# A two-block transformer forward pass: the order and the engine of the first grouped weight tiles' low parts, and the queue of the scratch writes

## The chip, the cores and the metric

The kernel runs as one program on one core of a Trainium2 chip. The metric is the device time of one execution in microseconds, as the median over several executions; lower is better.

## The reference

One sequence of 512 tokens with 1024 features passes through two blocks, all in float32.

```python
def first_block(x, c, ...):                     # two layers
    mod = silu(c) @ ada_w[layer] + ada_b[layer]           # six rows of shifts, scales, gates
    h = modulate(rms_norm(x, pre_mix_g), sh_m, sc_m)
    y = gmlp_mixer(h, ...)                                # layer 0: gelu, layer norm, causal 128x128 mixing
    y = fox_mixer(h, ..., k, v, dcum)                     # layer 1: 16 heads, causal, forget gates
    x = x + g_m * rms_norm(y, post_mix_g)
    h = modulate(rms_norm(x, pre_ffn_g), sh_f, sc_f)
    x = x + g_f * rms_norm(swiglu(h, w_gu, w_down), post_ffn_g)   # hidden width 2816
    # after layer 0: k, v, dcum = shared_kv(x, ...), one projection for the later layer

def second_block(x, p, w_in, ...):
    u = rmsnorm(x, norm_in)
    # one projection to: mLSTM q, k, v, o, z and gates; attention q, k, v, z; indexer q, k, weights
    hm = mlstm(...)                                       # 4 heads
    ha = dsa_attention(...)                               # 8 heads, keys chosen by the indexer's top 128
    h = x + concat(hm, ha) @ w_out
    h = h + (p @ w_ple) * sigmoid(h @ w_ple_gate)
    return rmsnorm(h, norm_final)
```

## The kernel before

Matrix products run in a rounded float32 format, and to keep the precision each operand is split into a high and a low part. ScalarE writes the high part of a weight tile (128x1024) as a rounded copy of the loaded tile `raw`, and another engine subtracts it from `raw` to get the low part (`wsplit`, lines 272 to 284). Each product is then three products on TensorE: high by high, high by low, low by high (`mm3`, lines 415 to 418). Which engine makes a low part follows from a running count of tiles: with `share` = 2 each second one goes to GpSimd, with 1 all, with 0 none; the others go to VectorE.

The activations h lie transposed, as 8 blocks of 128 features by 512 tokens, again as high and low parts. `gemm_a` multiplies a weight tile, held still, with h and gives 128 outputs by 512 tokens. `gemm_b` holds blocks of h still and gives 128 tokens by 512 outputs; it keeps four accumulators, one for each row block of 128 tokens. TensorE's sums lie in two sets of four banks, `acc` and `tp`.

At the end of a layer part `post` (lines 533 to 557) takes each row block's two accumulators, normalises, adds the residual, writes the new residual to memory, normalises again, and for each pair of row blocks `to_T` (lines 373 to 409) transposes the result into h for the next stage, block by block: a scaling on ScalarE (line 405 or 407), a rounding copy and a subtraction on VectorE (lines 408, 409). So the first 256 tokens of h are there before the last 256. The next `gemm_a` uses this at three places (both feed-forward blocks and the indexer projection `w_ix`): its first four weight tiles are a group, whose products are done first for tokens 0 to 255 of all four tiles, then for tokens 256 to 511 (`halves`, lines 427 to 438). Within a half, tile follows tile, and each tile runs all its k blocks with all three products. The low parts of these four tiles go to GpSimd (`gshare` = 1).

DMAs are all issued by SP, in one queue, in order: weight tiles into four `raw` buffers, rows that are broadcast, and writes and reads of scratch memory. Besides the residuals these are: the copies of x transposed for a later layer (`spill`, xT), the keys of the first attention as stacks of high and low halves (`spread`, four DMAs of 256 KB for each pair of heads), half of the values (line 1078), and the queries and keys of the second attention (lines 1271, 1272 and `spread`). They are loaded again when their heads come up.

The order of each engine's instructions is made by a planner, which takes the program's order as priority and its own costs as times. An instruction that waits stops what is queued behind it on its engine, and on SP its DMAs.

Of the kernel before, what the change touches and what calls it, by code (L numbers as in the profile page):

```python
# [20 lines left out]
P = 128  # L21
T_ = 512
NT = 4
# [168 lines left out]
def body(tc, nc, a):  # L192
    V, S_, G, PE = nc.vector, nc.scalar, nc.gpsimd, nc.tensor

    with ExitStack() as es:
# [176 lines left out]
        def to_T(ts, xn, g, sh, hi, lo, js=range(KD), spill=None):  # L372


            n = len(ts) * P
            c = slice(ts[0] * P, ts[0] * P + n)
            per = 512 // n
            for q, j in enumerate(js):
                if q % per == 0:
                    pt = tp()  # L380
                    f = None
                src = pt[:, (q % per) * n:(q % per + 1) * n]
                for i, t in enumerate(ts):
                    PE.transpose(src[:, i * P:(i + 1) * P], xn[t][j // 4][:, (j % 4) * P:(j % 4 + 1) * P], ident[:])  # L384
                if g is None:
                    S_.activation(hi[j][:, c], src, AF.Copy)
                    V.tensor_sub(lo[j][:, c], src, hi[j][:, c].bitcast(F32))
                    continue
                if spill is not None and q % per == per - 1:
                    raw, f = T(), T()  # L390
                    part = [(j - per + 1 + i, slice(i * n, (i + 1) * n)) for i in range(per)]
                    for i, s in part:
                        S_.activation(f[:, s], pt[:, s], AF.Identity, scale=g[:, i:i + 1], bias=sh[:, i:i + 1])
                    V.tensor_copy(raw, pt)
                    nc.sync.dma_start(spill[j - per + 1:j + 1, :, c].rearrange("j p n -> p j n"), b3(raw, per))
                    for i, s in part:
                        V.tensor_copy(hi[i][:, c], f[:, s])
                        V.tensor_sub(lo[i][:, c], f[:, s], hi[i][:, c].bitcast(F32))
                if spill is not None:
                    continue  # L400
                if f is None:
                    f = T()
                fj = f[:, (q % per) * n:(q % per + 1) * n]
                if sh is None:
                    S_.activation(fj, src, AF.Copy, scale=g[:, j:j + 1])
                else:
                    S_.activation(fj, src, AF.Identity, scale=g[:, j:j + 1], bias=sh[:, j:j + 1])
                V.tensor_copy(hi[j][:, c], fj)  # L408
                V.tensor_sub(lo[j][:, c], fj, hi[j][:, c].bitcast(F32))  # L409
# [10 lines left out]
        def gemm_a(h, w, n, evac, m=P, group=0, nfill=0, share=0, gshare=1):  # L420


            hi, lo = h
            i = 0
            while i < n:
                run = list(range(i, min(n, i + (group if i == 0 and group else 1))))
                halves = (slice(0, 256), slice(256, 512)) if i == 0 and group else (slice(0, 512),)
                ws, accs = [], []
                for q in run:
                    ws.append(wsplit(w[q], KD * m, gshare if len(run) > 1 else share))  # L430
                    accs.append(acc())
                    if len(run) == 1:
                        fill(nfill if i >= 10 or not group else 0)
                for c in halves:
                    for (wh, wl), pt in zip(ws, accs):
                        for k in range(KD):
                            mm3(pt[0:m, c], wh[:, k * m:(k + 1) * m], wl[:, k * m:(k + 1) * m],
                                hi[k][:, c], lo[k][:, c], k == 0, k == KD - 1)
                for q, pt in zip(run, accs):
                    evac(q, pt)  # L440
                i += len(run)
# [92 lines left out]
        def post(gb, xsrc, xdst, alloc, done):  # L534
# [4 lines left out]
            def evac(g, t, pt):  # L539
# [3 lines left out]
                if g == 1:  # L543
# [6 lines left out]
                    rsq(r, r, 1.0 / D)  # L550
                    for h in range(2):
                        V.scalar_tensor_tensor(xr[h], yg[t, h], r, xr[h], ALU.mult, ALU.add)
                        nc.sync.dma_start(xdst[rows, h * 512:(h + 1) * 512], xr[h])
                    xn = [yg[t, 0], yg[t, 1]]
                    norm_rows(xr, xn)
                    done(t, xn)
# [362 lines left out]
        def spread(d, at, hi, lo):  # L919

            for q, (src, half) in zip(at, ((hi, TOP), (lo, TOP), (hi, BOT), (lo, BOT))):
                nc.sync.dma_start(d[q].rearrange("(a p) n -> p a n", a=2),
                                  src[half].unsqueeze(1).broadcast_to((64, 2, 512)))

        def loader(alloc, src, n, last):

# [122 lines left out]
        with tc.tile_pool(name="x", bufs=1) as px:  # L1049
# [24 lines left out]
            def vdone(q, t, o):  # L1074
                if q < 2:
                    vt_[t, q] = o
                else:
                    nc.sync.dma_start(vscr[(q - 2) * NT + t], o.bitcast(F32))
            gemm_b(hk, a["w_k"], range(2), KD, headnorm(kt_, ka, kdone), head=True, share=KS, hshare=KH)
            dcol = []  # L1080
            dscr = scratch([16, 512])
# [115 lines left out]
        with tc.tile_pool(name="z", bufs=NZ) as pz:  # L1197
# [65 lines left out]
            def ev_a(i, pt):  # L1263
# [4 lines left out]
                if i % 2 == 0:  # L1268
                    for q, half in enumerate((TOP, BOT)):
                        ot = (BOT, TOP)[q]  # L1270
                        nc.sync.dma_start(d[3 * q, half], hi[half])
                        nc.sync.dma_start(d[3 * q, ot], lo[half])
                else:
                    spread(d, (1, 2, 4, 5), hi, lo)
            gemm_a(h, a["w_aqk"], 2, ev_a, share=2)
# [343 lines left out]
```

## Time and profile before

| | before |
|---|---|
| time, median of 3 runs | 1910.1 us (1907.51 to 1917.22) |
| profiled execution: its time | 1910.77 us |
| profiled execution: span | 1908.9 us |
| mean granted TensorE clock | 0.983 |
| VectorE busy | 1130.9 us (59%) |
| ScalarE busy | 792.2 us (41%) |
| GpSimd busy | 375.9 us (20%) |
| moved by DMA | 305.75 MB, all but some 1.5 MB on the one queue |

The span runs from the first instruction's start to the last one's end. A stretch is busy for an engine where an instruction of it runs; matmuls overlap, so their busy time is no measure of rate, and the number of matmuls in a stretch is counted as well. The granted clock is a share of TensorE's full speed.

### The profile page before, as it was taken

The page shows a single profiled execution, that of the slowest core. Times are in us where ns is not written, and L with a number is a line of the kernel's source. Part 1 is how long each engine was busy: PE and PEld are TensorE (multiplying, and loading weights), DVE is VectorE, ACT ScalarE, POOL GpSimd, SP SyncE. Part 2 cuts the span into 40 slices and gives each one's busy share as a digit, 9 for nine tenths or more (in the row PEclk, how much of TensorE's full clock was granted, in tenths as well). Part 3 has the DMA queues.
Part 4 walks back from the last instruction along what each step waited for, and adds up shares of the span by engine and source line. Part 5 has one row for each costly group of instructions (what it writes and reads, how often), then busy time and mean ns, then how long its engine had stood idle before and what let it go on. Part 6 is the DMA issues. An engine that isn't in the chain of part 4 may idle for free. (4 is left out here: it accounts for less than half of the span.)

```text
span 1908.9 us, 23835 instructions
## 1 busy us (share of the span) xinstructions
PE 1832.5 (96%) x8688; PEld 1514.8 (79%) x8688; DVE 1130.9 (59%) x2132; ACT 792.2 (41%) x1395; POOL 375.9 (20%) x216
## 2 busy tenths in 40 slices
PE   8899989999999999799998999999989999999998
PEld 5788877888888877587777888888878888888887
DVE  7879844677772256439876433232267978846534
ACT  5334324423232245448764422222246246455334
POOL 2100122222220012344323111100020363031011
PEclk9999999999999999899998999999989999999999
DMA  8684752477773444855533222222434744332522
GB/s 336 235 280 134 238 207 83 158 266 271 249 253 107 136 144 145 265 177 157 185 100 111 92 97 99 97 98 103 144 116 134 231 143 135 105 105 89 192 90 100
DMA packets 109647, 305.75 MB, mean 160 GB/s; under 512 B 12277, under 2 KB 15133, under 8 KB 109530
## 3 DMA queue, kind: packets, MB, share of 16 engines
q1 hardware_dynamic: 109530, 304.23, 47.8%
q8 instruction: 69, 1.13, 0.2%
q14 instruction: 48, 0.39, 0.1%
HBM read 269.50 MB, written 37.30 MB: 161 GB/s over the span
## 5 line engine op out<-in xcount | busy, mean ns | idle before, releaser
L279 ACT ACTIVATE whi<-raw 128x1024 fp32r<-128x1024 f32 x293 | 309.9, 1059 | 672.0 <-PE acc L418 295.9
L282 POOL TENSOR_TENSOR wlo<-raw,whi 128x1024 fp32r<-128x1024 f32 x124 | 305.2, 2465 | 1348.5 <-ACT whi L279 1062.2
L417 PE MATMUL acc<-h,whi 128*128 128x512 f32 (+1 forms) x1112 | 417.3, 375 | 10.4 <-DVE h L409 10.2
L416 PE MATMUL acc<-h,whi 128*128 128x512 f32 (+1 forms) x1112 | 417.6, 376 | 5.8 <-DVE h L408 5.2
L418 PE MATMUL acc<-h,wlo 128*128 128x512 f32 (+1 forms) x1112 | 416.0, 374 | 0.6 <-POOL wlo L282 0.6
L282 DVE TENSOR_TENSOR wlo<-raw,whi 128x1024 fp32r<-128x1024 f32 x169 | 214.4, 1271 | 299.2 <-ACT whi L279 294.7
L416 PE MATMUL acc<-whi,h 128*128 128x512 f32 x608 | 241.4, 398 | 19.5 <-ACT whi L279 12.2
L417 PEld LDWEIGHTS acc<-h,whi 128*128 128x128 f32 x1112 | 212.3, 191 | 48.2 <-DVE h L409 12.7
L416 PEld LDWEIGHTS acc<-h,whi 128*128 128x128 f32 x1112 | 212.4, 191 | 42.1 <-DVE h L408 6.0
L417 PE MATMUL acc<-wlo,h 128*128 128x512 f32 x608 | 240.0, 395 | 4.8 <-DVE wlo L282 3.3
L418 PEld LDWEIGHTS acc<-h,wlo 128*128 128x128 f32 x1112 | 212.4, 191 | 37.2 <-POOL wlo L282 1.0
L418 PE MATMUL acc<-whi,h 128*128 128x512 f32 x608 | 240.2, 395 | 0.0
L416 PE MATMUL acc<-whi,s 128*128 128x512 f32 (+1 forms) x488 | 190.5, 390 | 0.7 <-DVE t L1305 0.7
L302 DVE SCALAR_TENSOR_TENSOR raw<-raw,cact 128x1024 f32<-128x1024 f32 x96 | 146.7, 1535 | 74.8 <-DMA raw<-in_ada 68.2
L417 PE MATMUL acc<-wlo,s 128*128 128x512 f32 (+1 forms) x488 | 190.7, 391 | 0.0
L418 PE MATMUL acc<-whi,s 128*128 128x512 f32 (+1 forms) x488 | 190.2, 390 | 0.0
L416 PEld LDWEIGHTS acc<-whi,h 128*128 128x128 f32 x608 | 115.2, 190 | 44.3 <-ACT whi L279 12.6
L417 PEld LDWEIGHTS acc<-wlo,h 128*128 128x128 f32 x608 | 115.2, 190 | 29.2 <-DVE wlo L282 4.1
L418 PEld LDWEIGHTS acc<-whi,h 128*128 128x128 f32 x608 | 115.2, 190 | 26.0 <-DVE h L409 3.0
L416 PEld LDWEIGHTS acc<-whi,s 128*128 128x128 f32 x488 | 91.7, 188 | 20.0 <-DVE t L1305 1.1
L417 PEld LDWEIGHTS acc<-wlo,s 128*128 128x128 f32 x488 | 91.7, 188 | 18.8
L418 PEld LDWEIGHTS acc<-whi,s 128*128 128x128 f32 x488 | 91.7, 188 | 18.8
(349 smaller groups left out, 2395.4 us busy)
## 6 DMA issues: line engine op xcount, KB each, us to landing
raw<-in_ada SPq DMA_DIRECT2D x96, 512.0 KB, 3.7
raw<-in_w_gu SPq DMA_DIRECT2D x88, 512.0 KB, 3.7
raw<-in_w_dn SPq DMA_DIRECT2D x44, 512.0 KB, 3.2
scr<-t SPq DMA_DIRECT2D x72, 256.0 KB, 3.8
raw<-in_w_o SPq DMA_DIRECT2D x20, 512.0 KB, 3.3
row<-scr SPq DMA_DIRECT2D x36, 256.0 KB, 3.3
d<-in_ada SPq DMA_DIRECT2D x16, 512.0 KB, 5.5
raw<-in_w_v SPq DMA_DIRECT2D x16, 512.0 KB, 5.1
```

The lines of the kernel that those rows point to most:

```text
L279: S_.activation(hi[:, 0:n], raw[:, 0:n], AF.Copy)
L282: e.tensor_sub(lo[:, 0:n], raw[:, 0:n], hi[:, 0:n].bitcast(F32))
L302: V.scalar_tensor_tensor(raw, raw, 1.0, cact[0], ALU.mult, ALU.mult, accum_out=modc[:, col:col + 1])
L416: PE.matmul(out, lh, rh, start=start, stop=False)
L417: PE.matmul(out, lh, rl, start=False, stop=False)
L418: PE.matmul(out, ll, rh, start=False, stop=stop)
```

## The change

There are two parts.

In `gemm_a` the group of four tiles is written out by itself. All four tiles are loaded and their high parts made. Then, for tokens 0 to 255, the loop over k is the outer one and the tiles the inner: for each k block and tile the two products that need only the high part of the weights (high by high, high by low). After these, tile by tile, VectorE makes the tile's low part and TensorE adds the eight products with it. Tokens 256 to 511 follow in the same order, with the low parts already there. A bank's first product alone starts the sum. The group's tiles no longer advance the running count of `wsplit`. The tile after the group sums into a bank of `tp` instead of `acc`.

The writes of the residuals, of xT, of the keys, of the values and of the second attention's queries and keys are issued by GpSimd instead of SP.

```diff
-                    nc.sync.dma_start(spill[j - per + 1:j + 1, :, c].rearrange("j p n -> p j n"), b3(raw, per))
+                    nc.gpsimd.dma_start(spill[j - per + 1:j + 1, :, c].rearrange("j p n -> p j n"), b3(raw, per))
...
-                halves = (slice(0, 256), slice(256, 512)) if i == 0 and group else (slice(0, 512),)
                 ws, accs = [], []
-                for q in run:
-                    ws.append(wsplit(w[q], KD * m, gshare if len(run) > 1 else share))
-                    accs.append(acc())
-                    if len(run) == 1:
-                        fill(nfill if i >= 10 or not group else 0)
-                for c in halves:
-                    for (wh, wl), pt in zip(ws, accs):
+                if len(run) == 1:
+                    ws.append(wsplit(w[i], KD * m, share))
+
+                    accs.append(tp() if group and i == group else acc())
+                    fill(nfill if i >= 10 or not group else 0)
+                    for k in range(KD):
+                        mm3(accs[0][0:m], ws[0][0][:, k * m:(k + 1) * m], ws[0][1][:, k * m:(k + 1) * m],
+                            hi[k], lo[k], k == 0, k == KD - 1)
+                else:
+                    raws = []
+                    for q in run:
+                        accs.append(acc())
+                        raws.append(load_w(w[q], KD * m))
+                        ws.append([tile_of(pw, q_, F32R, 1024) for q_ in ("whi", "wlo")])
+                        S_.activation(ws[-1][0], raws[-1], AF.Copy)
+
+                    for nh, c in enumerate((slice(0, 256), slice(256, 512))):
                         for k in range(KD):
-                            mm3(pt[0:m, c], wh[:, k * m:(k + 1) * m], wl[:, k * m:(k + 1) * m],
-                                hi[k][:, c], lo[k][:, c], k == 0, k == KD - 1)
+                            for (wh, _), pt in zip(ws, accs):
+                                PE.matmul(pt[:, c], wh[:, k * P:(k + 1) * P], hi[k][:, c], start=nh == k == 0, stop=False)
+                                PE.matmul(pt[:, c], wh[:, k * P:(k + 1) * P], lo[k][:, c], start=False, stop=False)
+                        for (wh, wl), pt, raw in zip(ws, accs, raws):
+                            if nh == 0:
+                                V.tensor_sub(wl, raw, wh.bitcast(F32))
+                            for k in range(KD):
+                                PE.matmul(pt[:, c], wl[:, k * P:(k + 1) * P], hi[k][:, c], start=False,
+                                          stop=nh == 1 and k == KD - 1)
...
-                        nc.sync.dma_start(xdst[rows, h * 512:(h + 1) * 512], xr[h])
+                        nc.gpsimd.dma_start(xdst[rows, h * 512:(h + 1) * 512], xr[h])
...
-                nc.sync.dma_start(d[q].rearrange("(a p) n -> p a n", a=2),
-                                  src[half].unsqueeze(1).broadcast_to((64, 2, 512)))
+                nc.gpsimd.dma_start(d[q].rearrange("(a p) n -> p a n", a=2),
+                                    src[half].unsqueeze(1).broadcast_to((64, 2, 512)))
...
-                    nc.sync.dma_start(vscr[(q - 2) * NT + t], o.bitcast(F32))
+                    nc.gpsimd.dma_start(vscr[(q - 2) * NT + t], o.bitcast(F32))
...
-                        nc.sync.dma_start(d[3 * q, half], hi[half])
-                        nc.sync.dma_start(d[3 * q, ot], lo[half])
+                        nc.gpsimd.dma_start(d[3 * q, half], hi[half])
+                        nc.gpsimd.dma_start(d[3 * q, ot], lo[half])
```

## Rows read from the trace of the kernel before

**Rows 1.** The page: share of TensorE; then groups of instructions, busy us, mean ns.

```profile
PE 1832.5 (96%) x8688; PEld 1514.8 (79%) x8688; DVE 1130.9 (59%) x2132; ACT 792.2 (41%) x1395; POOL 375.9 (20%) x216
...
L282 POOL TENSOR_TENSOR wlo<-raw,whi 128x1024 fp32r<-128x1024 f32 x124 | 305.2, 2465 | 1348.5 <-ACT whi L279 1062.2
...
L282 DVE TENSOR_TENSOR wlo<-raw,whi 128x1024 fp32r<-128x1024 f32 x169 | 214.4, 1271 | 299.2 <-ACT whi L279 294.7
```

**Rows 2.** Stretches, us: length, then each engine's busy us (x instructions), clock, DMA share.

```profile
326.50:359.60 33.10, 28.54 (x210) 26.85 (x209) 24.86 (x42) 16.09 (x30) 10.73 (x5) 0.90 0.36 119
1030.60:1066.30 35.70, 29.36 (x209) 27.75 (x209) 25.27 (x43) 15.98 (x30) 10.41 (x5) 0.86 0.32 111
...
351.00:359.00 8.00, 8.00 (x69) 8.00 (x69) 5.35 (x4) 5.97 (x7) 2.41 (x1) 1.00 0.25 76
...
330.30:337.00 6.70, 4.73 (x18) 4.11 (x18) 6.23 (x10) 2.54 (x6) 4.05 (x2) 0.50 0.47 145
```

**Rows 3.** Timeline of VectorE in the first start: begin us, duration us, line, operation.

```profile
324.85 2.88 DVE L552 SCALAR_TENSOR_TENSOR s<-t,sm,s 128x512 f32<-128x512 f32 x1
327.65 2.60 DVE L409 TENSOR_TENSOR h<-t,h 128x256 fp32r<-128x256 f32 x1
330.17 2.43 DVE L408 CAST h<-t 128x256 fp32r<-128x256 f32 x1
332.52 0.74 DVE L552 SCALAR_TENSOR_TENSOR s<-t,sm,s 128x512 f32<-128x512 f32 x1
333.19 0.41 DVE L409 TENSOR_TENSOR h<-t,h 128x256 fp32r<-128x256 f32 x1
...
338.07 0.68 DVE L542 TENSOR_TENSOR t<-acc,gb 128x512 f32<-128x512 f32 x1
...
343.96 0.29 DVE L408 CAST h<-t 128x256 fp32r<-128x256 f32 x1 [0.62 <-ACT t L407]
```

**Rows 4.** Timeline of GpSimd in the first start.

```profile
324.72 7.73 POOL L282 TENSOR_TENSOR wlo<-raw,whi 128x1024 fp32r<-128x1024 f32 x3 [18.55 <-ACT whi L279]
```

**Rows 5.** Timeline of ScalarE in the first start: the fourth high part.

```profile
333.98 1.04 ACT L279 ACTIVATE whi<-raw 128x1024 fp32r<-128x1024 f32 x1
```

**Rows 6.** Timeline of TensorE, first start and key projection; in brackets idle before, releaser.

```profile
330.30 0.58 PE L417 MATMUL acc<-h,whi 128*128 128x256 f32 x1 [1.51 <-DVE h L409]
...
332.65 0.58 PE L416 MATMUL acc<-h,whi 128*128 128x256 f32 x1 [1.55 <-DVE h L408]
...
709.09 0.79 PE L417 MATMUL acc<-wlo,h 128*128 128x512 f32 x1 [1.95 <-DVE wlo L282]
```

**Rows 7.** Timelines of TensorE, ScalarE and VectorE in the value projection.

```profile
790.78 1.22 PE L416 MATMUL acc<-whi,h 128*128 128x512 f32 x2 [12.18 <-ACT whi L279]
...
789.67 1.06 ACT L279 ACTIVATE whi<-raw 128x1024 fp32r<-128x1024 f32 x1 [0.24 <-DMA raw<-in_w_vv]
...
770.53 0.42 DVE L1102 TENSOR_SCALAR q<-q 16x512 f32<-16x512 f32 x1
```

**Rows 8.** SP's queue: begin us, us to the last issue's end, DMA, number.

```profile
730.45 3.65 SPq L271 DMA_DIRECT2D raw<-in_w_vv  x3
737.29 41.27 SPq L922 DMA_DIRECT2D scr<-t  x32
...
783.52 10.30 SPq L271 DMA_DIRECT2D raw<-in_w_vv  x5
...
762.89 15.67 SPq L922 DMA_DIRECT2D scr<-t  x16
...
699.70 0.33 SPq L553 DMA_DIRECT2D scr<-s  x1
```

**Rows 9.** Stretches, as in rows 2: value projection, two for comparison.

```profile
778.30:803.50 25.20, 11.50 (x39) 8.60 (x38) 15.87 (x30) 13.90 (x21) 11.72 (x5) 0.66 0.78 271
762.00:778.00 16.00, 16.00 (x74) 13.27 (x74) 5.98 (x9) 6.33 (x8) 0.00 (x0) 1.00 0.80 221
1100.00:1200.00 100.00, 100.00 (x443) 82.84 (x442) 33.83 (x32) 28.97 (x38) 14.36 (x6) 1.00 0.29 95
```

## The prediction, made before the changed kernel ran

> **What bounds the kernel now.** I read the page's engine shares first: TensorE is busy 96% of the span [rows 1]. So only a stretch where TensorE waits, or runs at the lower of its two clocks, can give time back. Then the table of stretches, for the three places where a group of four weight tiles begins a stage (both feed-forward blocks and the indexer projection) [rows 2]. Each holds about 208 short products and transposes; the first takes 33.1 us, the other two 35.7 each. Where the same 256-column products run undisturbed, 69 take 8.00 us, 0.116 each, so 208 want 24.1 us. The excess is 9.0 + 11.6 + 11.6 = 32.2 us. Inside the first lie 6.7 us at a granted clock of 0.50, the 1.2 GHz level; the other two have such a spell as well.
>
> The timeline of VectorE in the first of them tells why [rows 3]. Three operations in a row take 2.88, 2.60 and 2.43 us; the same forms take 0.74, 0.41 and 0.29 a little later. In just that time GpSimd makes three low parts of the group, 7.73 us together [rows 4]. VectorE loses 2.14 + 2.19 + 2.14 = 6.5 us, so with the fourth low part about 8.6. ScalarE's squares wait for it, and behind them stands the copy of the fourth high part, which starts at 333.98 [rows 5]. TensorE meanwhile stands 1.51 and 1.55 us for VectorE's activation parts [rows 6].
>
> The one large wait of TensorE is elsewhere: 12.18 us, up to 790.78, for a high part in the value projection [rows 7]. SP's queue shows the cause: three loads of w_vv, then 32 writes of keys over 41.27 us, and only at 783.52 the other five loads [rows 8]; between them stand a write of the forget gate and eight reads of xT. The high part starts as its load lands [rows 7]. From 778.3 to 803.5 TensorE did 39 products, which at 443 per 100 us want 8.8 us: 16.4 us of excess, the wait and a mean clock of 0.66 [rows 9].
>
> **Part 1, the grouped tiles.** The products are the same in number and size (4 x 2 x 8 x 3 = 192), only in another order. What goes: 3 x 4 low parts of GpSimd. What comes: 12 low parts on VectorE, 1.27 us each [rows 1], 5.1 us per start, ready from the moment the high parts are. Without GpSimd's passes the first L552 in [rows 3] ends at 325.6 and the second about 327, so the squares and the four high parts follow one another on ScalarE and the fourth is ready near 329.8 (before: 335.0). TensorE enters the group at 326.5, needs all four within its first step of k, and so idles about 2.6 us; then 62 products run 7.2 us to 337.0 and the 32 with low parts 3.7 us to 340.7. The low parts are due from 337.0 on and have 7 us on a VectorE with gaps.
>
> What is late next: the other two row blocks. Now 5.9 us pass from the last block's L542 to its first activation part [rows 3]; without the 8.6 us that L542 can start near 330.4 instead of 338.07, so the part is there at 336.3, or at 341.4 if all four low parts stand ahead of it. TensorE asks for it at 340.7: 0 to 0.7 us. After that TensorE takes 0.93 us a step of k (8 products) and VectorE 0.7 (0.29 + 0.41): no more waits. I leave 2.6 + 0.5 us of waiting and 0.9 for a spell of low clock, 4.0 per start: 32.2 - 12.0 = 20 us won. Bounds: nothing won, if the 5.1 us hit the chain and the rest comes back as another wait; 32 with no wait left. The fifth tile gets a bank of the other set, so that it need not wait for the four accumulators that now end together; cost nothing, hidden behind its own 24 products.
>
> A side effect in the code: the grouped tiles no longer count in the turn that hands low parts to GpSimd. By lines 280 and 281 the first group of the key projection then gives one tile of four to GpSimd instead of two, and the second feed-forward block 14 instead of 13: GpSimd's low parts go from 124 to 112, VectorE's from 169 to 181. In the key projection that takes one of two slowdowns of VectorE away (2.1 us) and adds a 1.27; I count 0, and what can come back at most is a wait like the 1.95 us there for VectorE's low part [rows 6].
>
> **Part 2, the writes.** 112 DMAs move: 32 of residuals, 8 of spills, 32 of keys, 8 of values, 32 of the second attention's operands. SP then loads, apart from the small writes that stay (the gate's among them). In the value projection the fourth w_vv load can go as soon as its buffer is free; by the code that is when w_f, split beside the first key pairs near 740, is done with its own. The next limit is the gate's write, which holds SP until its source is there (770.5 + 0.4) [rows 7]; loads that come free before it can be out by then. So the 12.18 us and the low clock behind them go: 16.4.
>
> What takes their place is GpSimd's queue. All low parts of w_vv and w_q are made there, in turn with the writes. The second 16 key writes start at 762.89 and took 15.67 us on SP, 0.98 each [rows 8]. The fifth low part gets its buffer in the middle of them (the first w_vv tile is done at about 767) and is due one tile after the present wait begins, 778.4 + 24 x 0.227 = 783.9. If it comes behind all 16, TensorE waits where 762.9 + 16X + 2.4 passes 783.9, from X = 1.16 us per write. The trace has no DMA issued by GpSimd. From below, a plain write costs SP 0.33 us of queue [rows 8]; from above, a GpSimd pass over 128x1024 costs 2.47 [rows 1]. I take 1.2, near the 0.98 of these same writes: 0.6 us of wait. I count 15 of the 16.4; bounds 0 and 16.4, and worse in the other-side rival below.
>
> The other moved writes: residuals and spills stand on GpSimd's queue where, but for one key tile, it now has nothing else; each waits for VectorE there and holds only later low parts. The 8 values, some 8 us at 0.98, stand among low parts that come every 5.45 us and take 2.4, so 3 us are free per tile, and three tiles of lead cover the 8. The 32 operand writes come at four per tile of products, by 0.98 four of 5.45 us. I add 1 us for all of it, bounds -1 and +10.
>
> **Sum.** The profiled execution took 1910.8 us (span 1908.9), 0.7 above the median of 1910.1. 1910.8 - 20 - 15 + 1 = 1876.8, say 1877.
>
> **Rivals.**
> *GpSimd's queue is the new bound in the value projection.* At X = 2.0 the wait is 16 x 0.84 = 13.4 us and the second part wins nothing; with part 1 intact 1910.8 - 20 + 1 = 1892. For it: VectorE is busy 5.98 of 16.0 us there [rows 9]; if a write rests while VectorE works, 0.98 becomes 1.56, a wait of 6.4 us, and 1883. Against: three tiles of lead. The Trainium skill speaks for it: in "SBUF — State Buffer", section "SBUF: two separate sides", a DMA from GpSimd's queue has its descriptors written by that engine, which is locked out of the shared port while VectorE copies in a fast mode, and the advice is to issue from SP or ScalarE. The slowdowns of [rows 3] agree with a port held for a whole instruction; no row shows a descriptor being written. Chance 0.13.
>
> *The loads stay late.* SP keeps the order gate, xT, w_vv; the wait at 790 remains and only part 1 works: 1892. For it: that order now [rows 8]; against: three w_vv loads go even ahead of the writes. Chance 0.09.
>
> *The low parts land in VectorE's chain.* Then 5.1 us per start come off, 15 of the 20: 1892. For it: they are ready early and the engine is in order; against: VectorE waits for ScalarE several times in each block, and low parts fit there. Chance 0.11.
>
> *The other side: a write holds GpSimd and slows VectorE for as long as a low part does, 2.4 us.* Four residual writes in each start then replace the four low parts and cost the same 8.6 us, VectorE's own 5.1 come on top (3 x 5.1 = 15), and the value projection waits 16 x 1.24 = 20 us, 4 over its excess now: 1910.8 + 15 + 4 = 1930. It decides from where 12 writes in the starts and 16 in the value projection eat the 36 us: 12X + 16(X - 1.16) = 36, X = 1.95. Against: SP's writes cost a third to a half of that. Chance 0.09.
>
> **How the numbers follow.** Forecast 0.55, with its own range 1862 to 1890 (12 us less won, or the waits of part 1 gone too). The three middle cases 0.33, near 1892 alone and near 1907 two at once; the other side 0.09; better than 1862 0.03. The range 1862 to 1906 leaves out that 0.03 and, above, the other side and some of the pairs. A change under 0.5% (9.6 us) can't be told from none: faster is the forecast and most of the middle cases, 0.79; same 0.11, the pairs; slower 0.10.
>
> **What would show it.** VectorE's operations in the three starts back at 0.3 to 0.8 us; those stretches at 26 to 30 us; the fourth w_vv load before 771 and no wait over 3 us before the fifth tile's products; a mean granted clock above the 0.983 of now. Wrong would be: writes of 2 us on GpSimd, or low parts there that end after TensorE asks for them.

## The result and the profile after

The changed kernel takes 1891.0 us (median of 4 runs, 1888.4 to 1893.7) where the kernel before, beside it, takes 1912.3: a ratio of 0.9878, with a 95% interval of 0.9857 to 0.9898. The forecast was 1877. The gain is 21 us; the forecast, made against the profiled 1910.8, had 34.

The profiled execution took 1890.45 us, with a span of 1888.6 us and a mean granted clock of 0.989. Both kernels do the same 8,688 products and transposes in nearly the same order, so the time from the start of the n-th to that of the m-th compares a stage across traces. From the start times, in us (the row "end of the program" is from the end of ScalarE's last output scaling to the end of the span):

| stretch (n to m) | before | after | difference |
|---|---|---|---|
| first start, feed-forward 1 (1300 to 1500) | 39.9 | 32.2 | -7.7 |
| late tiles of feed-forward 1 (2100 to 2650) | 124.9 | 130.3 | +5.4 |
| down and key projection (2650 to 3190) | 125.1 | 122.5 | -2.6 |
| value projection (3190 to 3600) | 110.1 | 109.3 | -0.8 |
| second start, feed-forward 2 (4500 to 4800) | 55.3 | 45.2 | -10.1 |
| third start and the rest of the indexer (6250 to 6800) | 110.1 | 102.5 | -7.6 |
| end of the program | 3.8 | 6.7 | +3.0 |
| all other stretches together | | | +0.1 |

The sum is -20.3, the difference of the two spans. So the starts gave more than was forecast, and the value projection gave nothing.

The page of the kernel after answers to [rows 1]: GpSimd makes 112 low parts; VectorE's 169 and the group's 12 on a line of their own make 181.

```profile
PE 1823.4 (97%) x8688; PEld 1506.0 (80%) x8688; DVE 1116.9 (59%) x2144; ACT 789.8 (42%) x1395; POOL 409.1 (22%) x316
...
L282 POOL TENSOR_TENSOR wlo<-raw,whi 128x1024 fp32r<-128x1024 f32 x112 | 273.3, 2443 | 893.3 <-ACT whi L279 825.9
L282 DVE TENSOR_TENSOR wlo<-raw,whi 128x1024 fp32r<-128x1024 f32 x169 | 214.7, 1273 | 301.8 <-ACT whi L279 278.8
```

The table of stretches of the kernel after, columns as in [rows 2]: the three starts, and the value projection.

```profile
328.20:353.70 25.50, 25.45 (x210) 24.92 (x209) 16.78 (x41) 13.71 (x29) 3.15 (x4) 1.00 0.39 127
1026.50:1052.00 25.50, 25.46 (x209) 24.84 (x208) 16.80 (x40) 13.62 (x28) 4.02 (x4) 1.00 0.37 125
1391.70:1417.20 25.50, 25.50 (x210) 25.02 (x209) 17.25 (x41) 12.41 (x26) 3.13 (x4) 1.00 0.49 158
757.50:781.50 24.00, 9.41 (x30) 7.25 (x29) 11.88 (x13) 9.58 (x13) 20.26 (x21) 0.64 0.86 283
```

Each start is a solid 25.5 us at full clock, where [rows 2] has 33.1 and 35.7. VectorE's timeline in the first start (begin, duration) shows why: the forms that took 2.88 and 2.60 us in [rows 3] are back at 0.75 and 0.42, and the four low parts of 1.2 us lie between them.

```profile
326.54 0.75 DVE L568 SCALAR_TENSOR_TENSOR s<-t,sm,s 128x512 f32<-128x512 f32 x1
327.21 0.42 DVE L409 TENSOR_TENSOR h<-t,h 128x256 fp32r<-128x256 f32 x1
...
328.95 1.22 DVE L451 TENSOR_TENSOR wlo<-raw,whi 128x1024 fp32r<-128x1024 f32 x1
```

In the value projection the wait is still there, with another name. TensorE's timeline of the kernel after, to be read beside [rows 7]:

```profile
773.01 0.80 PE L417 MATMUL acc<-wlo,h 128*128 128x512 f32 x1 [14.59 <-POOL wlo L282]
```

GpSimd's timeline says what that low part waited for (in brackets: idle before, and what ended it):

```profile
735.31 4.78 POOL L938 DMA_DIRECT2D scr<-t  x8 [0.16 <-issue]
...
743.64 0.60 POOL L938 DMA_DIRECT2D scr<-t  x1 [1.85 <-DMA scr<-t]
...
758.73 0.60 POOL L938 DMA_DIRECT2D scr<-t  x1 [10.06 <-ACT t L1081]
...
769.99 0.60 POOL L938 DMA_DIRECT2D scr<-t  x1 [0.15 <-issue]
770.60 9.32 POOL L282 TENSOR_TENSOR wlo<-raw,whi 128x1024 fp32r<-128x1024 f32 x4
```

All 32 key writes stand ahead of the first low part of w_vv. A write holds the queue only 0.60 us, but the later ones of the first 16 wait until an earlier write has landed (0.24 to 1.85 us each), and the second 16 wait 10.06 us for their data. SP did what was forecast, up to a point: four w_vv loads went out by 737, but the other four again only at 784.79. Their buffers come free from 773.0 on, as the low parts are made, but reads of xT stand ahead of them on SP, and the last four of these waited for buffers of their own until 782.25. TensorE did not wait for these loads.

```profile
727.13 9.83 SPq L271 DMA_DIRECT2D raw<-in_w_vv  x4
...
782.25 2.45 SPq L1125 DMA_DIRECT2D t<-scr  x4
784.79 1.90 SPq L271 DMA_DIRECT2D raw<-in_w_vv  x4
```

### The profile page after: what moved, and what is told of

It reads as the page before. It is cut to its first block, busy times and chain, and to the rows that moved or that the text cites. A ratio compares the mean times of both kernels' runs of the same rounds, so it can differ in the third digit from the quotient of the medians.

```text
span 1888.6 us, 23901 instructions
## 1 busy us (share of the span) xinstructions
PE 1823.4 (97%) x8688; PEld 1506.0 (80%) x8688; DVE 1116.9 (59%) x2144; ACT 789.8 (42%) x1395; POOL 409.1 (22%) x316
## 5 line engine op out<-in xcount | busy, mean ns | idle before, releaser
L279 ACT ACTIVATE whi<-raw 128x1024 fp32r<-128x1024 f32 x281 | 296.7, 1058 | 661.4 <-PE acc L418 302.1
L282 POOL TENSOR_TENSOR wlo<-raw,whi 128x1024 fp32r<-128x1024 f32 x112 | 273.3, 2443 | 893.3 <-ACT whi L279 825.9
L418 PE MATMUL acc<-h,wlo 128*128 128x512 f32 x896 | 350.0, 391 | 3.0 <-DVE wlo L282 3.0
L416 PE MATMUL acc<-h,whi 128*128 128x512 f32 x896 | 350.8, 392 | 0.8 <-DVE s L903 0.5
L417 PE MATMUL acc<-h,whi 128*128 128x512 f32 x896 | 349.6, 390 | 0.0
L418 PEld LDWEIGHTS acc<-h,wlo 128*128 128x128 f32 x896 | 168.6, 188 | 40.2 <-DVE wlo L282 5.1
L416 PEld LDWEIGHTS acc<-h,whi 128*128 128x128 f32 x896 | 168.7, 188 | 36.9 <-issue 1.7
L302 DVE SCALAR_TENSOR_TENSOR raw<-raw,cact 128x1024 f32<-128x1024 f32 x96 | 151.6, 1589 | 76.6 <-DMA raw<-in_ada 75.2
L417 PEld LDWEIGHTS acc<-h,whi 128*128 128x128 f32 x896 | 168.5, 188 | 34.4
```

The source lines that it names most:

```text
L279: S_.activation(hi[:, 0:n], raw[:, 0:n], AF.Copy)
L282: e.tensor_sub(lo[:, 0:n], raw[:, 0:n], hi[:, 0:n].bitcast(F32))
L302: V.scalar_tensor_tensor(raw, raw, 1.0, cact[0], ALU.mult, ALU.mult, accum_out=modc[:, col:col + 1])
L416: PE.matmul(out, lh, rh, start=start, stop=False)
L417: PE.matmul(out, lh, rl, start=False, stop=False)
L418: PE.matmul(out, ll, rh, start=False, stop=stop)
```

## The experiments

Each run is compared with the kernel before on its own chip (1916 to 1917 us for e1 to e12, the 1912.3 above for the changed kernel). "Value stretch" and "late tiles" are the stretches of the table above; the undisturbed value stretch would be some 94 us, 110.1 less the 16.4 of [rows 9].

| run | ratio to before, 95% interval | value stretch | late tiles |
|---|---|---|---|
| changed kernel | 0.9878 (0.9857 to 0.9898) | 109.3 | 130.3 |
| e1 group only | 0.9885 (0.9859 to 0.9912) | 110.2 | 131.3 |
| e2 writes only | 1.0038 (1.0018 to 1.0057) | 108.3 | 129.1 |
| e3 w_vv's low parts on VectorE | 0.9868 (0.9844 to 0.9893) | 105.2 | 131.6 |
| e4 group's low parts on GpSimd | 1.0063 (1.0038 to 1.0088) | 108.4 | 132.6 |
| e5 keys written once, as e3 | 0.9827 (0.9802 to 0.9853) | 101.0 | 132.0 |
| e6 keys written once | 0.9839 (0.9822 to 0.9855) | 100.9 | 127.1 |
| e7 xT after values, as e3 | 0.9834 (0.9817 to 0.9852) | 103.2 | 133.8 |
| e8 columns from tile 6 | 0.9895 (0.9881 to 0.9910) | 108.8 | 134.4 |
| e9 xT read early, as e3 | 0.9796 (0.9778 to 0.9813) | 94.2 | 128.7 |
| e10 keys once, xT early | 0.9823 (0.9806 to 0.9841) | 101.6 | 129.3 |
| e11 as e10, low parts on VectorE | 0.9814 (0.9799 to 0.9828) | 96.2 | 131.0 |
| e12 as e9, fewer columns | 0.9924 (0.9900 to 0.9948) | 93.7 | 151.7 |

### The two parts apart

e1 takes the group and puts the writes back on SP; e2 is the kernel before with the writes on GpSimd.

```diff
# e1, at all six places
-nc.gpsimd.dma_start(...)
+nc.sync.dma_start(...)
```

> The changed kernel with all writes issued by SP again: part 1 alone. By the stretches of the changed kernel's trace against the one before, the three group starts gave 7.6 + 10.3 + 10.4 = 28.3 us, of which the later tiles of the first feed-forward block took 5.4 back and the end of the indexer projection 3.2, so part 1 is worth some 20 net. Theory (part 1 is right whole, part 2 gave nothing): 1891 +- 3, TensorE's wait of 12 us for a high part of w_vv is back near 770, the late waits for VectorE's low parts near 505 to 566 stay, since the loads of that block run at their own pace. Rival (the writes on GpSimd cost something elsewhere, and the late waits come from them): 1884 to 1886 and no waits there. Rival (the writes on GpSimd gave a share of the 21): 1895 or more.

> The kernel before with only the queue of the writes changed: part 2 alone. Theory (in the value projection the wait only changes its cause, from a late load to low parts that stand behind the 32 key writes on GpSimd's queue): 1909 to 1913, no difference from before that can be told; a wait of 13 to 16 us for GpSimd's low part near 765. Rival (the writes pay, but only because the low parts of the group no longer stand among them, or the reverse, they hold the group's low parts): the three starts change by more than 2 us each and the time leaves 1905 to 1917.

e1 measured 0.9885, the changed kernel 0.9878, with overlapping intervals: part 1 is the whole gain, as far as can be told, and part 2 on top of it nothing. TensorE's wait in the value projection is that of [rows 7] again:

```profile
792.06 1.22 PE L416 MATMUL acc<-whi,h 128*128 128x512 f32 x2 [12.05 <-ACT whi L279]
```

e2 is slower than before by 0.4%, not equal, and its value projection waits 14.3 us for GpSimd's low part, as expected. Of the rival there is something too: its first start grew by 2.6 us (42.5 against 39.9), the other two did not. It loses more in the late tiles (+4.2) and at the end of the program (+3.3), and wins 1.8 in the value projection. GpSimd's and TensorE's timelines of e2 in the first start:

```profile
327.07 2.47 POOL L282 TENSOR_TENSOR wlo<-raw,whi 128x1024 fp32r<-128x1024 f32 x1 [6.42 <-ACT whi L279]
330.38 0.56 POOL L553 DMA_DIRECT2D scr<-s  x1 [0.85 <-DVE s L552]
...
334.76 4.65 POOL L282 TENSOR_TENSOR wlo<-raw,whi 128x1024 fp32r<-128x1024 f32 x2
```

```profile
339.76 0.58 PE L417 MATMUL acc<-h,whi 128*128 128x256 f32 x1 [4.47 <-DVE h L409]
```

A residual write waits for VectorE, and the next low part, queued behind it, starts late and then slows VectorE late. The changed kernel avoids that because no low part of the group is on GpSimd's queue.

### The engine or the order of the products

```diff
-V.tensor_sub(wl, raw, wh.bitcast(F32))
+G.tensor_sub(wl, raw, wh.bitcast(F32))
```

> The changed kernel with the group's twelve low parts back on GpSimd, in the new order of the products (products with the low parts last). It tells the order from the engine. Theory (GpSimd's passes made VectorE's steps of 0.3 to 0.7 us last 2.4 to 2.9, and the starts waited for these): VectorE's steps in the starts are at 2.4 to 2.9 us again while GpSimd makes low parts, and 12 to 20 of the 28.3 us are lost: 1903 to 1911. Rival (the order is what counts: TensorE asks for the low parts later, so it does not matter who makes them): 1889 to 1894, the same as the changed kernel.

The whole gain is lost, and more: 1.0063, the first start at 42.8 us, the second at 55.8, the indexer at 113.6. VectorE's, GpSimd's and TensorE's timelines of e4:

```profile
328.69 2.90 DVE L568 SCALAR_TENSOR_TENSOR s<-t,sm,s 128x512 f32<-128x512 f32 x1
...
335.99 5.24 DVE L409 TENSOR_TENSOR h<-t,h 128x256 fp32r<-128x256 f32 x1
```

```profile
328.56 2.48 POOL L451 TENSOR_TENSOR wlo<-raw,whi 128x1024 fp32r<-128x1024 f32 x1 [6.42 <-ACT whi L442]
...
336.29 4.64 POOL L451 TENSOR_TENSOR wlo<-raw,whi 128x1024 fp32r<-128x1024 f32 x2
```

```profile
343.16 0.66 PE L384 MATMUL tp<-ident,t 128*128 128x128 f32 x2 [7.09 <-DVE t L370]
```

A step of 0.42 us lasts 5.24 while GpSimd makes two low parts, and ends 0.3 us after them. TensorE then waits 7.09 us for the chain behind that step. Residual writes stand between the low parts on GpSimd's queue here, as in e2, so e2 is the run to compare for the order alone: both have low parts and writes on GpSimd, and its starts take 42.5, 54.9 and 110.2 us, its ratio is 1.0038. The new order with GpSimd wins nothing on that. From e4 to the changed kernel only the engine differs, and the first start falls from 42.8 to 32.2. So in the new order the engine is what counts. Whether VectorE's low parts would give as much in the old order no run shows.

### What holds the value projection

e3 takes w_vv's low parts off GpSimd's queue.

```diff
-VS = 1
+VS = 0
```

> The changed kernel with the eight low parts of w_vv made by VectorE instead of GpSimd; everything else as changed. Theory (order on GpSimd's queue: the low parts wait behind 32 writes, each of which holds the queue only some 0.6 us, so a low part that is not on that queue is there when its high part is): the 14.6 us wait and the lower clock behind it go, 14 to 17 us, less 1 to 3 for eight passes of 1.2 us more on VectorE: 1875 to 1878. Rival (the loads stay late all the same, behind the gate's write on SP's queue): the wait comes back for a high part some 20 us later, 5 to 12 us, 1882 to 1890. Rival (VectorE is the bound there when it makes keys, values and low parts): waits for its low parts of over 5 us, 1885 or more.

The wait for the low part is gone, but the time hardly moves: 0.9868 against 0.9878, with overlapping intervals. The theory had 14 us more, and neither rival names what came. TensorE now waits 11.2 us for its accumulators, which ScalarE and VectorE copy out (v). TensorE's and ScalarE's timelines of e3:

```profile
792.92 0.77 PE L416 MATMUL acc<-whi,h 128*128 128x512 f32 x1 [11.21 <-DVE v L903]
```

```profile
779.40 0.82 ACT L1126 ACTIVATE t<-t,modc,gcol 128x512 f32<-128x512 f32 x1 [6.10 <-DMA t<-scr]
...
783.72 0.81 ACT L1126 ACTIVATE t<-t,modc,gcol 128x512 f32<-128x512 f32 x1 [1.21 <-DMA t<-scr]
...
787.64 0.36 ACT L901 ACTIVATE v<-acc 128x256 fp32r<-128x256 f32 x1
```

The copies (L901) are queued behind scalings of xT (L1126), and these wait for their reads. The table of stretches of e3, columns as before with the DMA share second to last, the line of its xT reads (KB, median us to landing) and SP's queue (begin, us to the last issue's end) bear on why the reads are late:

```profile
755.00:765.00 10.00, 10.00 (x52) 7.32 (x51) 9.22 (x14) 5.38 (x9) 2.59 (x5) 1.00 0.97 333
765.00:775.00 10.00, 10.00 (x46) 8.27 (x45) 5.18 (x8) 6.75 (x7) 5.88 (x10) 1.00 1.01 331
```

```profile
t<-scr SPq DMA_DIRECT2D x8, 256.0 KB, 9.0
```

```profile
762.52 0.37 SPq L1125 DMA_DIRECT2D t<-scr  x1
...
770.34 5.29 SPq L1125 DMA_DIRECT2D t<-scr  x3
...
781.47 4.63 SPq L1125 DMA_DIRECT2D t<-scr  x4
```

The 16 DMA engines are full, and a read takes 9.0 us (median of the three whose landing the trace shows). SP also issues the reads late: they stand behind weight loads, and their nine buffers `t` are shared with the keys that are being written (SP waits 5.6 us until VectorE has split earlier reads, 2.2 until key writes have landed). Two causes were set against each other: the bytes, or the order on ScalarE's queue. The late issue was not tried by itself. e5 and e6 cut the bytes: each key half is written once, 128 KB instead of 256, and read back twice.

```diff
-nc.gpsimd.dma_start(d[q].rearrange("(a p) n -> p a n", a=2),
-                    src[half].unsqueeze(1).broadcast_to((64, 2, 512)))
+nc.gpsimd.dma_start(kscr[pr, q], src[half])
...
-nc.sync.dma_start(got[p_][q].bitcast(F32), src[p_, q])
+for s in halves:
+    nc.sync.dma_start(got[p_][q].bitcast(F32)[s], src[p_, q])
```

> The kernel with w_vv's low parts on VectorE, and each key half written once (32 writes of 128 KB instead of 256) and read back twice, by 64 reads of 128 KB in place of 32 of 256: the bytes written fall by 4.2 MB, the bytes read stay. In the run with only the low parts moved, the DMA engines were busy 0.97 to 1.01 in each of the four slices from 745 to 785, the xT reads took 9.0 us to land, ScalarE's scalings of xT waited for them and TensorE waited 11.2 us for accumulators that are copied out behind these. Theory (the stretch is held by what the 16 DMA engines can move, 330 GB/s there): 4.2 MB less is 12.7 us less, so that wait falls below 3 us: ratio to the kernel before 0.977 to 0.982 (that of the run with the low parts alone was 0.987). Rival (an order on a queue, ScalarE's or SP's, holds the stretch whatever the bytes): the same wait within 3 us and 0.985 to 0.989. Rival (64 reads of 128 KB instead of 32 cost more on SP's queue, in the first attention): 0.987 or more, with new waits between 800 and 1020.

> The changed kernel with each key half written once, as in the run beside it, but w_vv's low parts still on GpSimd behind these writes. It tells the order on GpSimd's queue from the bytes. Theory (both: the writes hold the low parts because each waits until earlier ones have landed, 6.9 us apiece with 1.00 of the DMA engines busy): the writes go through in about half the time, the wait of 14.6 us for GpSimd's low part falls to 4 to 8 us: ratio 0.981 to 0.985. Rival (queue order alone; the low parts wait for the last key's data, not for the DMA engines): the wait stays over 11 us, 0.986 to 0.989. Rival (bytes alone): the wait is gone, 0.978 to 0.981, as good as the run beside it.

e5 took away only 4.5 of the 11.2 us: the same wait, 6.7 us, with the DMA share at 0.61 and 0.85 in the two stretches shown for e3. The theory of the bytes had put it below 3. e6 came out as expected in time, but not for the reason given: with smaller writes the planner put w_vv's first four low parts between the first and the second 16 writes, so order and bytes changed together. Its wait of 5.6 us is the one for the accumulators as well. GpSimd's timeline of e6:

```profile
738.25 2.08 POOL L1086 DMA_DIRECT2D scr<-t  x4 [0.84 <-DMA scr<-t]
740.35 2.40 POOL L282 TENSOR_TENSOR wlo<-raw,whi 128x1024 fp32r<-128x1024 f32 x1
...
758.82 4.19 POOL L1086 DMA_DIRECT2D scr<-t  x8
```

e7 tried the order by moving the reads and scalings of xT behind the value projection in the program.

```diff
-<the loop over j: read xT[j], scale, split>
 gemm_b(hk, a["w_vv"], ...)
+<the loop over j: read xT[j], scale, split>
```

> The kernel with w_vv's low parts on VectorE, full key writes, and the eight reads and scalings of xT put behind the value projection in the program, so that ScalarE's copies out of the accumulators no longer stand behind scalings that wait for a read. It tells the queue order on ScalarE from the bytes. Rival (order on ScalarE's queue): the wait of 11.2 us for the accumulators goes, 0.979 to 0.982. Theory (bytes: the DMA engines are full from 745 to 785 and something must come late): what is read late is late elsewhere, w_vv's later tiles or the query projection's operands, waits of 5 to 11 us in sum: 0.983 to 0.988.

It tells little: the planner still set the scalings between the copies, and TensorE waited 9.5 us for the accumulators, as ScalarE's timeline of e7 shows.

```profile
789.24 0.81 ACT L1127 ACTIVATE t<-t,modc,gcol 128x512 f32<-128x512 f32 x1 [2.90 <-DMA t<-scr]
789.96 0.36 ACT L901 ACTIVATE v<-acc 128x256 fp32r<-128x256 f32 x1
```

e9 takes away what the scalings wait for: xT is read before the key projection, into the buffers that later take the low part of the query operand. Low parts on VectorE, key writes full.

```diff
+hx = [[tile_of(px, "hm", F32R, bufs=16) for _ in range(KD)] for _ in range(2)]
+for j in range(KD):
+    nc.sync.dma_start(hx[1][j].bitcast(F32), xT[j])
 gemm_b(hk, a["w_k"], ...)
...
-    nc.sync.dma_start(f, xT[j])
-    S_.activation(f, f, AF.Identity, ...)
+    S_.activation(f, hx[1][j].bitcast(F32), AF.Identity, ...)
```

> The kernel with w_vv's low parts on VectorE and full key writes, but the eight reads of xT issued before the key projection, into the buffers of the query operand's low part; the scalings on ScalarE stay where they were. It tells whether the wait of 11.2 us near 781, for accumulators whose copies stand on ScalarE's queue behind scalings that wait for a read of xT, is one of that queue or of the bytes. By the stretch from product 3190 to 3600 (105.2 us in the run with the low parts alone, 109.3 in the changed kernel, 110.1 before), an undisturbed one would take 94. Theory (the reads land late because the DMA engines are full, and ScalarE's order hands that on to TensorE; read early, 2 MB leave the full stretch and nothing in front of the copies waits): no wait over 3 us from 735 to 805, the stretch at 94 to 97 us, ratio to the kernel before 0.978 to 0.982. Rival (bytes: something else of the 17 MB that stay comes late, a w_vv or w_q tile): a wait of 5 to 10 us for a high part, 100 to 105 us, 0.983 to 0.987.

This one shows what TensorE waits for. The value stretch is 94.2 us, with two waits of 2.0 us together, and the ratio 0.9796, faster than both kernels. The table of stretches of e9:

```profile
745.00:755.00 10.00, 10.00 (x46) 7.03 (x45) 6.43 (x9) 7.47 (x13) 0.60 (x1) 1.00 0.95 332
755.00:765.00 10.00, 10.00 (x52) 8.23 (x51) 8.72 (x13) 7.10 (x10) 4.78 (x8) 1.00 0.99 345
765.00:775.00 10.00, 10.00 (x46) 8.28 (x45) 8.65 (x17) 8.93 (x12) 5.12 (x8) 1.00 0.99 331
```

The DMA engines are as full as in e3 and the key writes as large, and TensorE does not wait in these 30 us. So full DMA engines are not what holds it: the late reads are, and the order on ScalarE's queue hands their lateness on, as its timeline of e3 shows. What made the reads late is not shown. e9 has SP issue them between 716.76 and 724.24, into other buffers, and so takes away the late issue and the slow landing at once.

e10 and e11 join both cures, with w_vv's low parts on GpSimd and on VectorE.

> The changed kernel (w_vv's low parts on GpSimd) with each key half written once and the xT reads issued before the key projection. Theory (the wait of 5.5 us that was left with the keys written once was only that of the late xT reads): stretch from product 3190 to 3600 at 94 to 97 us, no wait over 3 us from 735 to 805, ratio to the kernel before 0.977 to 0.981, some 1874 to 1880 where before has 1916. Rival (the low parts on GpSimd still come behind the key writes): a wait for GpSimd's low part of 3 us or more, 98 to 101 us, 0.982 to 0.984.

> As the run beside it (keys written once, xT read early), with w_vv's low parts on VectorE. Theory: once neither the writes nor the xT reads hold anything, it does not matter who makes these low parts: the stretch at 94 to 97 us and a time within 0.2% of the run beside it. Rival (eight passes of 1.2 us are too many for VectorE beside key and value work): a wait for VectorE's low part or for its copies of 2 us or more, 0.2 to 0.4% slower than the run beside it. Rival (the low parts on GpSimd slow VectorE there): 0.2 to 0.4% faster.

e10 has the rival's time (101.6 us, 0.9823) by another way. No low part comes late; TensorE waits 6.17 us for the accumulators. VectorE's and GpSimd's timelines of e10:

```profile
767.84 3.07 DVE L1131 CAST hm<-t 128x512 fp32r<-128x512 f32 x1 [0.28 <-ACT t L1130]
770.83 3.50 DVE L1132 TENSOR_TENSOR hm<-t,hm 128x512 fp32r<-128x512 f32 x2
```

```profile
768.19 2.42 POOL L282 TENSOR_TENSOR wlo<-raw,whi 128x1024 fp32r<-128x1024 f32 x1
```

It is the slowdown of the starts once more: a cast of 0.43 us lasts 3.07 beside a low part of GpSimd, and the copies of the accumulators stand behind these steps. In e11, without GpSimd's passes, the stretch is 96.2 us and the wait 2.8. The two times differ by 0.1%, which their intervals do not tell apart. With full writes and early reads e9 needs no smaller writes.

### The late tiles of the first feed-forward block

In the kernel after TensorE waits there for VectorE's low parts, which it never did in the trace of before. e8 begins the loads of the modulation columns earlier; e12 thins them out and moves the rest to the down projection.

```diff
# e8
-fill(nfill if i >= 10 or not group else 0)      # nfill = 2
+fill(nfill if i >= 6 or not group else 0)       # nfill = 1.8
# e12, on top of e9
-gemm_a(..., group=4, nfill=2, ...)
+gemm_a(..., group=4, nfill=1.5, ...)
-gemm_b((hh, hl), a[f"w_dn{l}"], ...)
+gemm_b((hh, hl), a[f"w_dn{l}"], ..., nfill=1)
```

> The changed kernel with the loads and passes for the modulation columns (two per weight tile from tile 10 on in the first feed-forward block) begun at tile 6 and thinned to 1.8 per tile, as many in all. Each pair of tiles with four such columns turned its four raw buffers round in 11.0 to 13.1 us, where TensorE needs 10.9; the head start that the earlier group gave TensorE is used up by 505. Theory (that cycle of four buffers, not the DMA engines at 0.73 to 0.83 nor the writes, takes back 5.4 of the 7.6 us won): the waits for VectorE's low parts from 505 to 566 go, 4 to 5 us: ratio 0.985 to 0.986 (the changed kernel's was 0.9878). Rival (the late low parts come from VectorE's own load or from slower loads at that time, whatever came before): the waits stay or move, 0.987 to 0.989.

> The fastest of the kernels so far (w_vv's low parts on VectorE, xT read early) with the modulation columns thinned in the first feed-forward block: 1.5 per weight tile from tile 10 on instead of 2, the rest, one per tile, in the down projection behind it. In ten runs the stretch from product 2100 to 2650 took 124.9 us before and 127.1 to 134.4 else, also where only the queue of the writes was changed (129.1), and beginning the columns earlier made it worse (134.4): so it is not the head start of the group that is given back. Theory (VectorE's low parts stand behind column passes that wait for a load into one of four shared buffers; with three columns per pair of tiles that cycle has slack): no wait for VectorE's low part over 0.5 us from 440 to 575, the stretch at 124 to 125.5, down from 128.7, ratio to the kernel before 0.977 to 0.979 (0.9796 without). Rival (DMA landing times of that moment, whatever the load): waits stay, 127 or more, 0.9796 or slower. Rival (the wait only moves to the down projection): the stretch from 2650 to 3190 grows from 123.4 to 126 or more, 0.979 to 0.981.

Both made it worse: 134.4 and 151.7 us. TensorE's waits from 440 to 575 in the kernel after, and from 440 to 590 in e12 (total us, times, longest):

```profile
PE acc L418 <- DVE wlo L282: 3.0, 5, 1.4
```

```profile
PE acc L418 <- DVE wlo L282: 17.2, 11, 2.2
```

With fewer loads (a DMA share of 0.60 from 500 to 560, against 0.77 in the kernel after) the low parts came later still. But neither run gave the cycle of four buffers slack. SP's waits from 440 to 560, in the kernel after and in e12, show that the loads of weight tiles (L271) now stand still for buffers that column passes (L302) hold:

```profile
SPq L271 <- DVE raw L302: 2.4, 1, 2.4
```

```profile
SPq L271 <- DVE raw L302: 38.9, 9, 6.6
```

In e8 it is 30.9 us. So both changes made that cycle slower, the forecasts of both fail, and whether its lack of slack costs the 5.4 us is not shown either way.

## Why the prediction was right in direction and wrong in size

**Part 1** was right, and its term too small. Forecast were 4.0 us of excess left per start; it is 25.5 - 24.1 = 1.4. The waits of 2.6 us for the four high parts and 0.5 for the other row blocks never came. That makes 28 us over three starts; the end of the indexer projection took 2.6 of it back (a wait of 1.90 us for ScalarE's copy at 1427, and 3.4 us at a granted clock of 0.50 from 1430.8), so 25.4 in the table. The mechanism, GpSimd's passes stretching VectorE's steps, is shown by e4. The rival "the low parts land in VectorE's chain" did not happen. One subtraction in the working is off (338.07 less 8.6 is 329.5, not 330.4); nothing hung on the 0.9 us.

**Part 2, the value projection, is the step that failed.** The prediction said: "The fifth low part gets its buffer in the middle of them", and asked only from what price of a write that one would be late. It took for granted that the first four low parts run ahead of the second 16 writes, as nothing stood between them when the writes were on SP. The planner put all 32 writes ahead, and the first low part ran at 770.60. The price was not the question: 0.60 us against the 1.2 taken and the threshold of 1.16. The 16.4 us were then lost to a wait of 14.6 us and a low clock behind it. The rival "GpSimd's queue is the new bound" has the right place and, by chance, the right time (1892), with a price of 2.0 that never was. The total meets it only because the 5.4 us that the starts gave beyond the forecast and the 5.4 that the late tiles took cancel out.

Even a right order on GpSimd would not have given the 15 us: e6 has it, with smaller writes, and its stretch takes 100.9. e3 shows the next wait, of 11.2 us, for accumulators behind late reads of xT, and e9 that the 15 us are there once these are early too: 109.3 - 94.2 = 15.1. Behind the wait that the change was to remove stood two more.

Beside this rival the Trainium skill was cited, "SBUF — State Buffer", section "SBUF: two separate sides": GpSimd can't write the descriptors of its DMAs while VectorE copies in a fast mode. The traces agree, in a small way, though no row names the mode. In the kernel after the key write issued at 766.41 held the queue 0.70 us instead of 0.60, until 0.125 us after a cast of VectorE. In e12, whose timelines of GpSimd and VectorE follow, the first of two writes held it 1.36 us, until 0.124 us after the second of two casts.

```profile
799.01 1.97 POOL L938 DMA_DIRECT2D scr<-t  x2 [0.47 <-DMA scr<-t]
```

```profile
799.50 0.74 DVE L1128 CAST hm<-t 128x512 fp32r<-128x512 f32 x2
```

Eleven key writes of all traces ended so, 0.10 to 0.13 us after a cast. Few writes meet a cast, so the medians hide it: the 24 writes of L938 in the kernel after with VectorE busy for over 80% of their time held the queue 606 ns, the 18 with under 20% 603 ns. It is 0.1 us of the 14.6.

**The other moved writes** were put at +1 us. While they run they cost nothing that can be seen. At the end of the program they cost 3.0 us, a term that the sum did not have. The chain of waits and ScalarE's timeline end with this scaling in the kernel before, the kernel after and e1:

```profile
1904.39 0.72 ACT s L1542
```

```profile
1881.13 0.72 ACT s L1558
```

```profile
1890.73 0.72 ACT L1558 ACTIVATE s<-s,sm 128x512 f32<-128x512 f32 x1 [0.29 <-DVE sm L1549]
```

The spans end at 1908.9, 1888.6 and 1895.2: 3.8, 6.7 and 3.8 us later. In the traces of e2 to e12 it is 6.7 to 7.2. Only the two kernels without DMAs on GpSimd have the shorter end.

**The key projection** was put at 0 and gave 2.6 us; the wait of 1.95 us for VectorE's low part [rows 6] is gone.

**The late tiles** were not in the prediction: +5.4 us. Their cause stays open. The kernel after and all twelve others have 127.1 us or more there, also e1 and e2 with one part each, so no part of the change can be named. Only one profile of the kernel before was taken, and that execution (1910.77 us) was a short one: of the 41 others on which the comparisons rest, 1907.5 to 1921.4 us, 4 were shorter. So the 124.9 may itself be a low value.

## What to carry to other kernels

When a queue gets new entries, write down the order in which the planner will put them beside what is there, before asking for their price; a cheap entry that waits is as dear as what it waits for. Before counting a wait as won, look for what is late next on every engine that must finish before TensorE goes on: here a load, a low part and a copy stood one behind another, each hiding the next. Work on GpSimd is paid by VectorE wherever VectorE's steps are on the path, as in the starts and in e10, so move passes off GpSimd in just those stretches.

## What the runs showed of the hardware that was not expected

- A DMA write holds GpSimd's queue for 0.53 to 0.73 us in the kernel after (medians by line), and it can be longer where a cast of VectorE runs in it: 0.70 us instead of 0.60 there, 1.36 in e12.
- Residual writes landed in 2.5 us from GpSimd (kernel after), in 2.1 and 2.9 from SP (before, e1), as medians. Key writes landed in 6.9 from GpSimd (kernel after; 8.3 in e3 with the DMA engines full) and in 3.8 from SP (before). GpSimd issued the second 16 key writes in 11.9 us, SP in 15.67, so the queue and the closer issue are not told apart.
- In all twelve traces with DMAs on GpSimd the program ended 3.0 to 3.4 us later after ScalarE's last scaling than in the two without.
- The 16 DMA engines can be busy for 0.95 to 0.99 of 30 us, at 331 to 345 GB/s, without a wait of TensorE (e9).
- One VectorE step can be held for two GpSimd passes in a row: 5.24 us instead of 0.42 (e4).
